# Forgetting attention with keys on the partitions, in slots with a written order on TensorE

## The chip, the cores and the metric

The kernel runs on one core of one Trainium2 chip. The metric is the device time of one execution in microseconds (us). A profile of one more execution tells, for each engine, when every instruction ran. The engines are TensorE (PE; its weight loads stand apart as PEld), VectorE (DVE), ScalarE (ACT), GpSimd (POOL) and SyncE (SP), which issues the DMA transfers.

## The reference, cut to what matters

One layer of a hybrid encoder, all in float32: 2048 positions, width 1024. A projection of the normalised input feeds three branches (forgetting attention, a state-space layer, attention into 256 memory tokens). Each is gated, projected back to 1024, and the three are merged with sigmoid gates; an output projection, the residual and a last norm follow. The change concerns the forgetting attention (12 heads of 64) and the merges.

```python
def forgetting_attention(q, k, v, log_f):
    F = jnp.cumsum(log_f, axis=1).transpose(0, 2, 1)
    ...
        s = jnp.einsum('bhqd,bhkd->bhqk', qi, kh)
        s = s + Fi[..., None] - F[:, :, None, :]
        s = jnp.where(key_pos[None, :] <= qpos[:, None], s, NEG)
        p = jax.nn.softmax(s, axis=-1)
        return jnp.einsum('bhqk,bhkd->bhqd', p, vh)
...
    gates = jax.nn.sigmoid(gl + b_merge[l]).reshape(Bn, L, N_BRANCH, D_MODEL)
    merged = (gates[:, :, 0] * (y_fox @ w_proj_fox[l])
              + gates[:, :, 1] * (y_s5 @ w_proj_s5[l])
              + gates[:, :, 2] * (y_mem @ w_proj_mem[l]))
```

The term F of the query is the same for all keys of a row, so softmax cancels it; only minus F of the key has to be added to the scores. Keys above the diagonal are masked.

## The kernel before, in words

Every product is made in float32 accuracy out of fp32r matmuls. `mm3` splits both factors into a high and a low part and makes three matmuls (lines 147 to 149). `split` makes the parts: high on POOL (line 893), or on ACT (line 891) once `hi_act` is set, and low on DVE (line 895). `load_w` loads a weight tile and splits it. Intermediate results go to DRAM and are loaded again, all by SP's queue.

The program has three stretches. `proj` makes all projections, the state-space and memory branches, and the gates of the first two chunks (a chunk is 512 positions, c = 0 to 3). Then comes attention (`gen_fox`) with a filler under it. Then the rest of the merges and the output projection (`merge_out`).

Attention before works with queries on the partitions. It goes through pairs of query blocks (head h, G = 7 to 0, 256 queries), in an order that mixes the small pairs of one head with the large ones of the next. `fox_scores` makes, for each block of 128 queries, the scores against up to 512 keys at a time with two matmuls (lines 751 and 752): the high and the low part of q against a tile that holds the high part of k in its upper 64 rows and the low part in its lower ones. One DVE operation (line 753) adds `nf` (minus F, broadcast over the partitions by a DMA), writes the row to SBUF and gives its maximum; POOL has added the mask into `nf` before (line 739). Then ACT takes the exponential with the row's sum (line 758), DVE the reciprocal (759), and POOL scales the row (762).

`fox_pv` does the pair before. TensorE transposes each 128x128 block of the row (line 783), ACT and DVE split what comes out into high and low (786 and 787; 791 and 792 on the diagonal), and a matmul of width 512 (line 799) multiplies both parts with a tile of values that holds high and low side by side. Lines 802 to 807 add the four quarters and multiply with the gate `gf`.

The filler is a generator that does six matmuls a step: first the gates of chunks 2 and 3 (`gen_gl`), then the merge of chunk 3 (`gen_merge0`), first its part without the attention's result, then, once `ready` is set, the part with it. `run` takes 0.355 of a step per step of attention, and holds it back behind a value matmul of eight steps before (`issue_after`). The Tile framework's scheduler otherwise orders the instructions of each engine by its own estimate of times, in the program's order where it can. What the filler has not done goes on after attention. `merge_out` then merges chunks 2, 1 and 0 with POOL adds on lines 997 and 998 (in `gen_merge0` the add is on line 963), and makes the output projection.

PSUM's eight banks are shared in this stretch as A 3, B 3, C 1 and F 1 (F is the filler's).

Of the kernel before, what the change touches and what calls it, by code (L numbers as in the profile page):

```python
# [33 lines left out]
PB, PBS = 4, 4  # L34
KS = 3
DUE = 6.0
QB = 2
PN = 768
# [11 lines left out]
class Layer:  # L50
# [17 lines left out]
    def setup(self):  # L68
# [19 lines left out]
        for n, sh, dt in (  # L88
            ("qh", [DF, L], F32), ("ql", [DF, L], F32), ("kh", [DF, L], F32), ("kl", [DF, L], F32),
            ("vs", [H, 16, 128, 128], F32), ("gf", [DF, L], F32), ("gs", [DF, L], F32),  # L90
            ("gl", [3 * D, L], F32), ("gm", [DM, L], F32), ("qmh", [DM, L], F32), ("qml", [DM, L], F32),
            ("u", [6, 8, 128, 256], F32), ("kd", [48, 16, 128], F32), ("nf", [H, L], F32), ("yx", [DF, L], F32), ("yc", [6, 8, 128, 256], F32),
            ("ys", [DF, L], F32), ("ym", [DM, L], F32), ("mp", [D, CW], F32), ("mg", [D, L], F32),
            ("mkh", [128, HM, ML], F32), ("mkl", [128, HM, ML], F32),
            ("mvh", [128, 2, DM], F32), ("mvl", [128, 2, DM], F32),
        ):
            s[n] = self.dram("s_" + n, sh, dt)
        self.s = s

    def constants(self):  # L100
# [6 lines left out]
        nc.sync.dma_start(out=self.bm, in_=i["b_merge"])  # L107
        self.bf = c.tile([H, 1], F32, name="bf")
# [35 lines left out]
    def mm3(self, out, a, b, first, last):  # L144

        nc = self.nc
        nc.tensor.matmul(out, a[0], b[0], start=first, stop=False)  # L147
        nc.tensor.matmul(out, a[0], b[1], start=False, stop=False)  # L148
        nc.tensor.matmul(out, a[1], b[0], start=False, stop=last)  # L149
# [106 lines left out]
    def proj_v(self, g, p):  # L256
# [6 lines left out]
        for t in range(16):  # L263
# [7 lines left out]
            o = self.ev.tile([128, 4, 128], F32R, tag="ehi", name="ev_v", bufs=2)  # L271
            pv = ps[:, :256].rearrange("p (h d) -> p h d", h=4)
            nc.scalar.copy(o[:, :, 0:64], pv)
            nc.vector.tensor_sub(o[:, :, 64:128], pv, fl32(o[:, :, 0:64]))
            nc.sync.dma_start(out=s["vs"][g * 4:(g + 1) * 4, t].rearrange("h p d -> p h d"), in_=fl32(o))
# [12 lines left out]
    def forget(self, p):  # L288
# [10 lines left out]
        nc.sync.dma_start(out=self.s["nf"], in_=e)  # L299
# [94 lines left out]
    def gen_gl(self):  # L394
        for n in range(len(TILES) - 24, len(TILES)):
            w = self.w_tile(n)
            for c in (2, 3):
# [6 lines left out]
                self.proj_chunk(*TILES[n], w, c, ps)  # L404
                yield
# [297 lines left out]
    def open_fox(self):  # L703
        self.fp, self.close_fp = self.pool("foxh", side="right")
        self.k0, self.q0 = [self.fox_keys(0, 0), self.fox_keys(0, 1)], self.fox_q(0, 3)

    def fox_keys(self, h, c):

        nc, s, p = self.nc, self.s, self.fp
        r, ks = slice(h * DH, (h + 1) * DH), slice(c * 1024, (c + 1) * 1024)  # L710
        kk = p.tile([128, 1024], F32R, tag="kk", name="kk", bufs=3)
        v = p.tile([128, 8, 128], F32R, tag="v", name="v", bufs=3)
        nf = p.tile([128, 1024], F32, tag="nf", name="nf", bufs=3)
        nc.sync.dma_start(out=fl32(kk[0:64]), in_=s["kh"][r, ks])
        nc.sync.dma_start(out=fl32(kk[64:128]), in_=s["kl"][r, ks])
        nc.sync.dma_start(out=nf, in_=s["nf"][h:h + 1, ks].partition_broadcast(128))
        nc.sync.dma_start(out=fl32(v), in_=s["vs"][h, c * 8:(c + 1) * 8].rearrange("t p d -> p t d"))
        return kk, v, nf

    def fox_q(self, h, c):  # L720
        nc, s, p = self.nc, self.s, self.fp
        r, cs = slice(h * DH, (h + 1) * DH), slice(c * 512, (c + 1) * 512)
        q = []
        for n in ("qh", "ql"):
            t = p.tile([128, 512], F32R, tag=n, name=n, bufs=QB)
            for a in range(2):
                nc.sync.dma_start(out=fl32(t[a * 64:(a + 1) * 64]), in_=s[n][r, cs])
            q.append(t)
        return q

    def fox_scores(self, p, hd, q, G, P):


        nc = self.nc
        for b in (1, 0):
            qb = 2 * G + b
            nk = 128 * (qb + 1)
            diag = hd[qb // 8][2][:, qb % 8 * 128:(qb % 8 + 1) * 128]
            nc.gpsimd.tensor_add(diag, diag, self.mask)
            qs = slice(qb % 4 * 128, (qb % 4 + 1) * 128)  # L740
            pr = p.tile([128, L // 2], F32, tag="Ps", name="Ps", bufs=PBS) if G < 4 else \
                p.tile([128, L], F32, tag="P", name="P", bufs=PB)
            nch = (nk + 511) // 512
            mx = p.tile([128, 4], F32, tag="mx", name="mx", bufs=4)
            for c in range(nch):
                w = min(512, nk - c * 512)
                wm = max(w, 256)
                kk, _, nf = hd[c // 2]
                c0 = c % 2 * 512
                ps = self.psA()  # L750
                nc.tensor.matmul(ps[:, :wm], q[0][:, qs], kk[:, c0:c0 + wm], start=True, stop=False)  # L751
                nc.tensor.matmul(ps[:, :wm], q[1][:, qs], kk[:, c0:c0 + wm], start=False, stop=True)  # L752
                nc.vector.tensor_tensor_reduce(  # L753
                    out=pr[:, c * 512:c * 512 + w], in0=ps[:, :w], in1=nf[:, c0:c0 + w], scale=1.0,
                    scalar=-3.0e38, op0=ALU.add, op1=ALU.max, accum_out=mx[:, c:c + 1])
            nm, den, rd = (p.tile([128, 1], F32, tag=n, name=n, bufs=4) for n in ("nm", "den", "rd"))
            nc.vector.reduce_max(nm, mx[:, :nch], axis=AX.X, negate=True)
            nc.scalar.activation(pr[:, :nk], pr[:, :nk], AF.Exp, bias=nm, accum_out=den)
            nc.vector.reciprocal(rd, den)  # L759
            for a in range(0, nk, PN):  # L760
                c = pr[:, a:min(a + PN, nk)]
                nc.gpsimd.tensor_scalar(out=c, in0=c, scalar1=rd, scalar2=0.5, op0=ALU.mult, op1=ALU.mult)  # L762
            P[b] = pr
            yield

    def fox_pv(self, p, h, hd, G, P):

        nc, s = self.nc, self.s
        po = self.psC()
        cs = slice(G * 256, (G + 1) * 256)  # L770
        r = slice(h * DH, (h + 1) * DH)
        gf = p.tile([64, 256], F32, tag="gf", name="gf", bufs=2)
        nc.sync.dma_start(out=gf, in_=s["gf"][r, cs])
        for kp in range(G + 1):
            ps = self.psB()
            t = p.tile([128, 2, 512], F32R, tag="Pt", name="Pt", bufs=3)
            hi, lo = t[:, :, 0:256], t[:, :, 256:512]
            for a in range(2):
                kt = 2 * kp + a
                for b in range(2):  # L780
                    if kt <= 2 * G + b:
                        o = a * 256 + b * 128
                        nc.tensor.transpose(ps[:, o:o + 128], P[b][:, kt * 128:(kt + 1) * 128], self.ident)  # L783
            psv = ps.rearrange("p (a n) -> p a n", a=2)
            if kp < G:
                nc.scalar.copy(hi, psv)  # L786
                nc.vector.tensor_sub(lo, psv, fl32(hi))  # L787
            else:
                for a in range(2):
                    c = slice(a * 128, 256)  # L790
                    nc.scalar.copy(hi[:, a, c], psv[:, a, c])
                    nc.vector.tensor_sub(lo[:, a, c], psv[:, a, c], fl32(hi[:, a, c]))
            for a in range(2):
                kt = 2 * kp + a
                v = hd[kt // 8][1][:, kt % 8, :]
                o, m = po, t[:, a, :]
                if kt == 2 * G + 1:
                    o, m = (z.rearrange("p (x b n) -> p x b n", x=2, b=2)[:, :, 1, :] for z in (o, m))
                self.pe = nc.tensor.matmul(o, v, m, start=(kt == 0), stop=(kt == 2 * G + 1))  # L799
            yield  # L800
        t = p.tile([128, 256], F32, tag="ot", name="ot", bufs=1)
        nc.scalar.copy(t, po[:, 256:512])
        nc.vector.tensor_add(t, po[:, 0:256], t)  # L803
        o = p.tile([64, 256], F32, tag="oo", name="oo", bufs=2)
        nc.scalar.copy(o, t[64:128])
        nc.gpsimd.tensor_add(o, o, t[0:64])
        nc.gpsimd.tensor_mul(o, o, gf)
        nc.sync.dma_start(out=s["yx"][r, cs], in_=o)

    def gen_fox(self):  # L810


        p, self.close_f = self.pool("fox", side="right")
        own = lambda h, a, b: [(h, G) for G in range(a, b, -1)]
        seq = own(0, 7, 7 - KS)
# [345 lines left out]
```

## Time and profile before

| | us |
|---|---|
| median of three runs | 3036.81 |
| lowest and highest | 3033.26, 3038.91 |
| the profiled execution's own time | 3032.29 |
| its span, first to last instruction | 3030.5 |
| PE, DVE, ACT, POOL busy | 2956.7, 1842.2, 1044.1, 864.8 |
| first score matmul (line 751) starts at | 1589.0 |
| last value matmul (line 799) starts at | 2513.4 |

A row of the profile names the engine, the line of the program, the operation, what it writes and reads, its shape and how often it ran; then the busy time, the mean time of one in ns, the idle time of the engine just before it, and what ended that idle time. A busy time is a union: two matmuls that overlap in the pipeline count once. A matmul's length includes its way through the array, so the price of one in a row of many is the distance between two starts. Rows of a single line's or tile's view give the shortest, median and longest time of one. The mean granted clock of TensorE was 0.992.

### The profile page before, as it was taken

How to read it: one execution, taken by the hardware profiler on the slowest of the kernel's cores; microseconds unless marked ns; L12 is line 12 of the kernel's file. 1: busy time of each engine (PE TensorE's matmuls, PEld its weight loads, DVE VectorE, ACT ScalarE, POOL GpSimd, SP SyncE). 2: the span in 40 equal slices, each digit the busy share in tenths (PEclk: the TensorE clock that was granted, in tenths of full speed). 3: DMA queues.
4: the chain of work that ended last, by engine and by line, in shares of the span. 5: the costliest groups of instructions: out<-in, count | busy, mean ns of one | idle time of the engine just before them, and what ended most of it. 6: DMA issues, size and time to landing. Idle time of an engine off the chain costs nothing.

```text
span 3030.5 us, 43647 instructions
## 1 busy us (share of the span) xinstructions
PE 2956.7 (98%) x14656; PEld 2424.2 (80%) x14656; DVE 1842.2 (61%) x4982; ACT 1044.1 (34%) x2049; POOL 864.8 (29%) x1160
## 2 busy tenths in 40 slices
PE   9999999999999999999999999999999897999999
PEld 7889977777777778888878888888888786788787
DVE  5333399899896673322216777777777875554444
ACT  5102111111112231222215666666666563332222
POOL 0010000000002342112215665565665662222100
PEclk9999999999999999999999999999999999999999
DMA  5343323323334655344352433444443548776542
GB/s 169 108 126 107 106 87 106 126 87 116 122 130 150 175 167 172 105 135 132 116 167 87 123 116 112 117 119 118 126 119 114 172 123 264 226 244 209 175 146 98
DMA packets 306671, 417.80 MB, mean 138 GB/s; under 512 B 84084, under 2 KB 165236, under 8 KB 306436
## 3 DMA queue, kind: packets, MB, share of 16 engines
q1 hardware_dynamic: 306160, 414.95, 44.9%
q8 instruction: 116, 1.90, 0.3%
q14 instruction: 107, 0.88, 0.1%
q10 hardware_dynamic: 288, 0.07, 0.0%
HBM read 276.00 MB, written 138.90 MB: 137 GB/s over the span
## 4 chain that ended last, share of the span: by engine, by line
PE 80%; DMA 9%; DVE 5%; issue 3%; POOL 2%; ACT 1%; SPq 0%; DVEq 0%; POOLq 0%; ACTq 0%
PE psF L147 10%; PE psF L148 10%; PE psF L149 10%; PE psA L149 8%; PE psA L147 8%; PE psA L148 8%; PE psC L799 6%; PE psB L783 5%; PE psA L752 3%; PE psA L751 3%; PE psC L147 2%; PE psC L149 2%; PE psC L148 2%; DMA wraw<-in_w_out 1%; DMA yr<-s_ys 1%
## 5 line engine op out<-in xcount | busy, mean ns | idle before, releaser
L147 PE MATMUL psF<-hh,whi 128*128 128x512 f32 (+1 forms) x1160 | 468.2, 404 | 5.5 <-DVE elo L228 2.5
L149 PE MATMUL psF<-hh,wlo 128*128 128x512 f32 (+1 forms) x1160 | 459.5, 396 | 0.0
L148 PE MATMUL psF<-hl,whi 128*128 128x512 f32 (+1 forms) x1160 | 459.1, 396 | 0.0
L893 POOL TENSOR_SCALAR whi<-wraw 128x1024 fp32r<-128x1024 f32 (+2 forms) x134 | 137.0, 1023 | 710.3 <-PE psA L148 307.0
L147 PE MATMUL psA<-hh,whi 128*128 128x512 f32 (+1 forms) x816 | 322.6, 397 | 2.5 <-POOL whi L893 1.5
L148 PE MATMUL psA<-hl,whi 128*128 128x512 f32 (+1 forms) x816 | 323.9, 397 | 0.0
L149 PE MATMUL psA<-hh,wlo 128*128 128x512 f32 (+1 forms) x816 | 321.8, 395 | 0.8 <-DVE wlo L895 0.8
L895 DVE TENSOR_TENSOR wlo<-wraw,whi 128x1024 fp32r<-128x1024 f32 (+2 forms) x168 | 204.9, 1221 | 191.8 <-POOL whi L893 152.5
L799 PE MATMUL psC<-Pt,v 128*128 128x512 f32 x864 | 266.1, 398 | 6.8 <-DVE ot L803 3.4
L787 DVE TENSOR_TENSOR Pt<-psB,Pt 128x512 fp32r<-128x512 f32 x336 | 226.4, 686 | 75.7 <-ACT Pt L786 73.2
L147 PEld LDWEIGHTS psF<-hh,whi 128*128 128x128 f32 x1160 | 218.6, 188 | 52.2 <-DVE elo L228 3.2
L149 PEld LDWEIGHTS psF<-hh,wlo 128*128 128x128 f32 x1160 | 218.4, 188 | 51.3 <-DVE wlo L895 0.4
L148 PEld LDWEIGHTS psF<-hl,whi 128*128 128x128 f32 x1160 | 218.7, 189 | 45.7 <-issue 0.4
L753 DVE CUSTOM_DVE_ANT_0 P<-psA,nf 128x512 f32<-128x512 f32 (+1 forms) x336 | 201.3, 627 | 45.7 <-PE psA L752 25.4
L786 ACT CAST Pt<-psB 128x512 fp32r<-128x512 f32 x336 | 191.7, 585 | 97.3 <-PE psB L783 52.4
L762 POOL TENSOR_SCALAR P<-P,rd 128x768 f32<-128x768 f32 (+1 forms) x240 | 192.1, 815 | 61.5 <-DVE rd L759 40.6
L751 PE MATMUL psA<-kk,qh 128*128 128x512 f32 (+1 forms) x480 | 185.1, 391 | 3.4 <-DVE mx L753 1.6
L147 PEld LDWEIGHTS psA<-hh,whi 128*128 128x128 f32 x816 | 154.0, 189 | 38.0 <-POOL whi L893 1.9
L149 PEld LDWEIGHTS psA<-hh,wlo 128*128 128x128 f32 x816 | 154.4, 189 | 35.9 <-DVE wlo L895 1.2
L148 PEld LDWEIGHTS psA<-hl,whi 128*128 128x128 f32 x816 | 154.4, 189 | 33.4
L799 PEld LDWEIGHTS psC<-Pt,v 128*128 128x128 f32 x864 | 153.8, 190 | 33.7 <-DVE Pt L787 5.6
L783 PE MATMUL psB<-ident,P 128*128 128x128 f32 x1200 | 176.3, 273 | 0.3
(373 smaller groups left out, 6243.1 us busy)
## 6 DMA issues: line engine op xcount, KB each, us to landing
wraw<-in_w_in SPq DMA_DIRECT2D x90, 512.0 KB, 4.1
s_gl<-ehi SPq DMA_DIRECT2D x96, 256.0 KB, 2.6
g<-s_gl SPq DMA_DIRECT2D x96, 256.0 KB, 4.6
wraw<-in_w_proj SPq DMA_DIRECT2D x40, 320.0 KB, 4.0
s_vs<-ev_v SPq DMA_DIRECT2D x48, 256.0 KB, 2.7
nf<-s_nf SPq DMA_DIRECT2D x24, 512.0 KB, 6.6
v<-s_vs SPq DMA_DIRECT2D x24, 512.0 KB, 6.1
qh<-s_qh SPq DMA_DIRECT2D x96, 128.0 KB, 3.7
```

The lines of the kernel that those rows point to most:

```text
L147: nc.tensor.matmul(out, a[0], b[0], start=first, stop=False)
L148: nc.tensor.matmul(out, a[0], b[1], start=False, stop=False)
L149: nc.tensor.matmul(out, a[1], b[0], start=False, stop=last)
L751: nc.tensor.matmul(ps[:, :wm], q[0][:, qs], kk[:, c0:c0 + wm], start=True, stop=False)
L753: nc.vector.tensor_tensor_reduce(out=pr[:, c * 512:c * 512 + w], in0=ps[:, :w], in1=nf[:, c0:c0 + w], scale=1.0, scalar=-3.0e38, op0=ALU.a ...
L762: nc.gpsimd.tensor_scalar(out=c, in0=c, scalar1=rd, scalar2=0.5, op0=ALU.mult, op1=ALU.mult)
L783: nc.tensor.transpose(ps[:, o:o + 128], P[b][:, kt * 128:(kt + 1) * 128], self.ident)
L786: nc.scalar.copy(hi, psv)
L787: nc.vector.tensor_sub(lo, psv, fl32(hi))
L799: self.pe = nc.tensor.matmul(o, v, m, start=(kt == 0), stop=(kt == 2 * G + 1))
L893: self.nc.gpsimd.tensor_scalar(out=hi, in0=x, scalar1=sc, scalar2=1.0, op0=ALU.mult, op1=ALU.mult)
L895: self.nc.vector.tensor_sub(lo, x, fl32(hi))
```

## The change

Attention is written anew, with keys on the partitions. A unit is a head and a chunk of 512 queries; the units go from chunk 3 to chunk 0, and through all heads in each. A slot is one tile of 128 keys of a unit: 16, 12, 8 or 4 slots a unit, 480 in all, and 13 more at the end.

In each slot two matmuls make the scores of 128 keys against up to 512 queries (`fox_score`). ACT copies them out of PSUM with minus F of the key added as its bias into a tile `T` (four key tiles each, six buffers), and DVE keeps a running maximum over the key tiles, from PSUM; on the diagonal POOL adds the mask to `T`, and DVE takes the maximum from there. When a unit's scores are done, four transposes and a DVE reduction give the maximum of each query (`fox_max`), ACT spreads it, and four more transposes put it on all partitions (`rows`, a PSUM bank of its own). Then `fox_exp`, two key tiles at a time: DVE adds the negated maximum from PSUM, ACT takes the exponential, POOL adds each tile to a running sum `acc`. `fox_pv` multiplies the exponentials with the values, in plain float32 (no split), the key tiles taking turns between the lower and the upper 64 partitions of the result. Four matmuls with a column of ones make the sums of each query out of `acc` (`fox_den`), and `fox_end` applies their reciprocals and the gate.

What follows a unit's scores is put at fixed slots behind them (`at`), so it runs between the scores of the next units. Every PE instruction of attention and filler goes through `te`, which chains it behind the one before in the order of the program. The filler now does the gates of chunks 2 and 3 and both parts of the merges of chunks 3 and 2, 0.67 steps a slot; chunk 2 waits until its 24 units are done. Weight tiles are loaded one ahead. `merge_out` keeps chunks 1 and 0. Minus F is transposed once (`forget`) and stays in SBUF; values are no longer split. The PSUM banks become A 2, B 1, C 2, F 2 and M 1.

```diff
-PACE, LAG = 0.355, 8
+PACE = 0.67
-PS2 = {"A": 3, "B": 3, "C": 1, "F": 1}
+PS2 = {"A": 2, "B": 1, "C": 2, "F": 2, "M": 1}
...
+    def te(self, op, *a, **k):
+        f = getattr(self.nc.tensor, op)
+        if not self.chain:
+            return f(*a, **k)
+        with self.tc.issue_after(self.pe.ins) if self.pe else nullcontext():
+            self.pe = f(*a, **k)
...
+    def fox_score(self, p, u, kt):
...
+        self.te("matmul", ps[:, w:], kk[:, ks], q[0][:, w:], start=True, stop=False)
+        self.te("matmul", ps[:, w:], kk[:, ks], q[1][:, w:], start=False, stop=True)
+        nc.scalar.activation(t[:, a:], ps[:, a:], AF.Identity, bias=bias)
+        if j >= 0:
+            nc.gpsimd.tensor_add(t[:, a:a + 128], t[:, a:a + 128], self.mask)
+            if kt:
+                nc.vector.tensor_max(mx[:, a:], mx[:, a:], t[:, a:])
+            else:
+                nc.vector.tensor_copy(mx, t)
+        elif kt:
+            nc.vector.scalar_tensor_tensor(out=mx, in0=ps, scalar=bias, in1=mx, op0=ALU.add, op1=ALU.max)
+        else:
+            nc.vector.tensor_scalar(out=mx, in0=ps, scalar1=bias, scalar2=None, op0=ALU.add)
...
+    def fox_exp(self, p, u, g, i):
...
+        if g < c:
+            t = tg[:, i:i + 2, :]
+            nc.vector.tensor_add(t, m.unsqueeze(1).to_broadcast([128, 2, CW]), t)
+            nc.scalar.activation(t, t, AF.Exp)
+        for e in (i, i + 1):
+            t, a = tg[:, e, :], 128 * e if g == c else 0
+            if g == c:
+                nc.vector.tensor_add(t[:, a:], m[:, a:], t[:, a:])
+                nc.scalar.activation(t[:, a:], t[:, a:], AF.Exp)
+            if g or e:
+                nc.gpsimd.tensor_add(acc[:, a:], acc[:, a:], t[:, a:])
+            else:
+                nc.gpsimd.tensor_copy(acc, t)
...
+        for kt in range(4 * g, 4 * g + 4):
+            t, a = u["T"][g][:, kt % 4, :], max(kt - 4 * c, 0) * 128
+            o = u["po"][64 * (kt % 2):64 * (kt % 2) + 64, a:]
+            self.te("matmul", o, u["v"][:, kt, :], t[:, a:], start=kt < 2, stop=kt >= 4 * c + 2)
...
+        for b in range(4):
+            self.te("matmul", pd[:, b:b + 1], u["acc"][:, b * 128:(b + 1) * 128], self.ones, start=True, stop=True)
...
+        seq = [(h, c) for c in range(NC - 1, -1, -1) for h in range(H)]
...
+            at = lambda d, f, *a: due.setdefault(slot - 1 + d, []).append(lambda: f(*a))
+            at(1, self.fox_values, p, u)
+            at(2, self.fox_max, p, u)
+            at(4, rows, u)
+            for g in range(c + 1):
+                for i in range(2):
+                    at(4 + 4 * g + 2 * i, self.fox_exp, p, u, g, 2 * i)
+                at(9 + 4 * g, self.fox_pv, u, g)
+            at(11 + 4 * c, self.fox_den, p, u)
+            at(13 + 4 * c, self.fox_end, p, u)
...
     def gen_merge0(self):
...
+        slabs = [(c, m, a) for c in (3, 2) for b in ((0, 1), (2,)) for m in range(KD) for a in b]
...
+        for _ in range(8):
+            yield
+        for c in (3, 2):
...
+                if part == 0 and c == 2:
+                    while self.done < 2 * H:
+                        yield
...
     def merge_out(self):
...
-        for c in range(NC - 2, -1, -1):
+        for c in (1, 0):
...
-        for n, _ in enumerate(fox):
-            marks.append(self.pe)
+        for _ in fox:
             due += PACE
             while due >= 1.0:
                 due -= 1.0
...
+                next(fill, None)
```

More of the change, by code (lines that the diff above doesn't have):

```diff
@@ L1 @@
+from contextlib import nullcontext
 import concourse.bass as bass
@@ L144, in mm3 @@
     def mm3(self, out, a, b, first, last):
[L146 to L149, printed above, removed]
+        self.te("matmul", out, a[0], b[0], start=first, stop=False)
+        self.te("matmul", out, a[0], b[1], start=False, stop=False)
+        self.te("matmul", out, a[1], b[0], start=False, stop=last)
+    def te(self, op, *a, **k):
[4 more added lines that the diff above has]
+            self.pe = f(*a, **k)
     def rsqrt(self, p, out, ssq, n):
@@ L298, in forget @@
         nc.vector.tensor_tensor_scan(e, one.to_broadcast([H, L]), z, 0.0, ALU.mult, ALU.subtract)
-        nc.sync.dma_start(out=self.s["nf"], in_=e)
+        pz = self.psB()
+        for t in range(16):
+            nc.tensor.transpose(pz[:, t * H:(t + 1) * H], e[:, t * 128:(t + 1) * 128], self.ident[0:H, 0:H])
+        nc.scalar.copy(self.nf, pz[:, :16 * H].rearrange("p (t h) -> p t h", h=H))
     def proj_kv(self, p):
@@ L720, in fox_q @@
[L720 to L725, printed above, removed]
-            for a in range(2):
[L727 to L787, printed above, removed]
-            else:
[L789 to L806, printed above, removed]
@@ new lines, in fox_rows @@
+    def fox_rows(self, u, ps, n):
+        for b in range(4):
+            self.te("transpose", ps[:n, b * 128:(b + 1) * 128], u["x"][:, b, :n], self.ident)
+        return ps
+    def fox_exp(self, p, u, g, i):
+        nc, c = self.nc, u["c"]
+        tg = u["T"][g]
+        if g == 0 and i == 0:
+            u["acc"] = p.tile([128, CW], F32, tag="acc", name="acc", bufs=2)
+        acc, m = u["acc"], u["m"]
+        if g < c:
[11 more added lines that the diff above has]
+                nc.gpsimd.tensor_copy(acc, t)
@@ L845, in gen_fox @@
+        while due:
+            run()
+            slot += 1
             yield
@@ L913, in merge_gate @@
         return t
-    def merge_w(self, m, part, pool=None):
-        return [self.load_w(self.i["w_proj"][2 * m + a], (5, 128)) for a in range(2)] if part == 0 else \
-            [self.load_w(self.i["w_proj_x"][m], (6, 128))]
     def merge_ws(self, m, p):
@@ L1074, in run @@
                 due -= 1.0
-                if n >= LAG and marks[n - LAG] is not None:
-                    with self.tc.issue_after(marks[n - LAG].ins):
-                        next(fill, None)
-                else:
-                    next(fill, None)
-        self.over = self.hi_act = True
+                next(fill, None)
+        self.hi_act = True
         for _ in fill:
             pass
+        self.chain = False
         self.close_f()
```

244 lines of the change are left out of this document (142 added, 102 removed).

## Prediction, made before the changed kernel was run

> **What bounds the kernel now.** I read the page's busy times first, then the busy times of three stretches of the span, then single stretches of time for the price of each kind of matmul.
>
> ```profile
> span 3030.5 us, 43647 instructions
> PE 2956.7 (98%) x14656; PEld 2424.2 (80%) x14656; DVE 1842.2 (61%) x4982; ACT 1044.1 (34%) x2049; POOL 864.8 (29%) x1160
> 0.00:1589.00 1589.00, 1564.91 (x7744) 1281.84 (x7744) 902.11 (x2527) 327.94 (x648) 212.94 (x307) 0.99 0.42 129
> 1589.00:2520.00 931.00, 914.81 (x4898) 760.68 (x4899) 688.06 (x2045) 579.23 (x1164) 563.26 (x800) 0.99 0.42 122
> 2520.00:3031.00 511.00, 476.93 (x2015) 381.64 (x2014) 251.99 (x411) 136.97 (x237) 88.64 (x55) 0.98 0.61 194
> ```
>
> The last three rows give, after each stretch's length, the busy time of PE, PEld, DVE, ACT and POOL, then clock and DMA. The stretches are what comes before attention (1589 us, which the change hardly touches), attention with the fill under it (931 us), and what is left of the merges with the output projection (510.5 us to the end). PE is busy almost throughout all three, so I count the change in PE time first and then ask whether another engine takes over. In attention DVE is at 74% and POOL at 60%.
>
> **Prices on PE.** A busy time overlaps its neighbours, so I take prices from the distance of starts.
>
> ```profile
> 2012.56 1.55 PE L799 MATMUL psC<-Pt,v 128*128 128x512 f32 x6
> 2018.37 0.60 PE L783 MATMUL psB<-ident,P 128*128 128x128 f32 x4
> 405.35 0.48 PE L149 MATMUL psA<-hh,wlo 128*128 128x512 f32 x1
> 405.76 1.08 PE L586 MATMUL psC<-u,m1t 128*64 128x256 f32 x8
> 406.78 0.33 PE L551 MATMUL psB<-ident,m1i 128*128 128x128 f32 x1
> 418.14 0.60 PE L626 MATMUL psC<-u,m 128*128 128x256 f32 x2
> 418.58 0.59 PE L627 MATMUL psC<-hs,z 128*128 128x256 f32 x2
> L799 PE MATMUL psC<-Pt,v 128*128 128x512 f32 x768 | 240.3, 408 | 6.8 <-DVE ot L803 3.4 <-DVE Pt L787 2.9 <-DVE Pt L792 0.2
> L799 PE MATMUL psC<-Pt,v 128*128 128x256 f32 x96 | 30.0, 313 | 0.0
> L783 PE MATMUL psB<-ident,P 128*128 128x128 f32 x1200 | 176.3, 273 | 0.3
> L783 PE MATMUL psB<-ident,Ps 128*128 128x128 f32 x432 | 65.9, 272 | 0.1
> ```
>
> A 512-wide fp32r matmul costs (1.55-0.39)/5 = 0.233 us, with 0.39 the length of one; a transpose (0.60-0.27)/3 = 0.11 us. A plain fp32 matmul leaves two records: two of 256 columns take 418.58-418.14 = 0.44 us, 0.217 each. The S5 block on L586 is four fp32 matmuls (eight records) whose outputs alternate between the lower and upper 64 partitions, which is the form of the new value product. One after another they would be 8 x 0.217 = 1.74 us. From the end of the matmul before (405.83) to the end of the block (406.84) it took 1.01 us, and the transpose behind it 0.26 instead of 0.11. So neighbours in different halves run together: 0.86 us of work and 0.30 us for entering and leaving.
>
> The Trainium skill (TensorEngine Tiling (Array Packing), Key Properties) says that a change of tiling mode drains TensorE. With no drain the sum below would be 36 us lower; the trace's 0.30 us per block agrees with the page.
>
> **PE time out and in.** Out: 768 value matmuls x 0.233 + 96 half-wide ones x 0.12 = 190 us, and 1632 transposes x 0.11 = 178 us. Scores stay: 80 matmuls a head with the same widths, only their operands swap sides. In, for each of 48 units (head h, 512 queries c): value products in groups of four key tiles. A full group is four steps of 0.433 (twice 0.217) + 0.30 = 2.03 us; a diagonal group, whose widths are 512, 384, 256 and 128, is 2 x 0.433 + 2 x 0.217 + 0.30 = 1.60. With 72 full and 48 diagonal groups: 223 us. Twelve transposes a unit: 576 x 0.11 = 63 us. Four one-column denominator matmuls a unit, which no row shows: not below one transpose (0.11), not above a two-record matmul (0.43); I take 0.22, two 128-column passes, as the weight load must still pass: 192 x 0.22 = 42 us (21 to 83). In total 368 out, 328 in: 40 us less.
>
> Merges moved under attention:
>
> ```profile
> 2520.00:3031.00 511.00, 266.66 (x671) 127.43 (x671) 0.98 0.61 194
> 2520.00:3031.00 511.00, 266.65 (x672) 127.75 (x671) 0.98 0.61 194
> 2520.00:3031.00 511.00, 264.96 (x672) 127.59 (x672) 0.98 0.61 194
> PE psA L147 <- ACT whi L891: 8.0, 1, 8.0
> PE psB L147 <- ACT ymg L891: 5.4, 3, 2.9
> PE psC L147 <- DVE g L996: 4.8, 2, 4.2
> ```
>
> The first three rows are lines 147, 148 and 149 in the last stretch: 2015 matmuls. Chunks 1 and 0 need 2 x 384 and the output 768, so 1536 stay and 479 move: 479 x 0.233 = 112 us. Moving does not shorten them. The last three rows are the largest waits of that stretch, at the start of the merges and at a change of chunk. I keep them whole: the new merge_out opens its buffers only when attention's are closed, so its first weights and y tiles still have to land and be split (minus 15 to plus 10 us). Last stretch: 510.5-112 = 398.5. Attention, if PE alone sets it and stalls stay as they are: 931-40+112 = 1003. With 1589 that is 2990.5, 40 us under the span. The 16 small transposes in forget (1.8 us) and the dropped value splitting (DVE, beside PE) I cost at nothing: PE is busy for 1565 of 1589 us there and covers them; uncovered they would be 2 us.
>
> **What POOL and DVE get.** The new path puts one running sum per key tile on POOL, 128x512, two inputs.
>
> ```profile
> 2599.51 0.82 DVE L895 TENSOR_TENSOR wlo<-wraw,whi 128x640 fp32r<-128x640 f32 x1
> 2600.25 1.93 DVE L895 TENSOR_TENSOR lob<-raw,hib 128x640 fp32r<-128x640 f32 x1
> 2599.68 1.82 POOL L997 TENSOR_TENSOR g<-g 128x512 f32<-128x512 f32 x1 [30.59 <-DVE g L996]
> 2841.05 1.29 POOL L997 TENSOR_TENSOR g<-g 128x512 f32<-128x512 f32 x1 [5.64 <-DVE g L996]
> L806 POOL TENSOR_TENSOR oo<-oo,ot x96: 714/731/1715, 1627.1 to 2517.9; 64x256 f32<-64x256 f32 x96
> L739 POOL TENSOR_TENSOR nf<-nf,mask x192: 444/459/1437, 1550.6 to 2495.7; 128x128 f32<-128x128 f32 x192
> L893 POOL TENSOR_SCALAR ymg<-yr x10: 607/618/1099, 2354.6 to 2382.4; 128x512 fp32r<-128x512 f32 x10
> L893 POOL TENSOR_SCALAR whi<-wraw x134: 714/1046/1798, 9.2 to 2483.0; 128x1024 fp32r<-128x1024 f32 x96, 128x768 fp32r<-128x768 f32 x24, 128x640 fp32r<-128x640 f32 x14
> L895 DVE TENSOR_TENSOR ymg<-yr,ymg x64: 674/693/2861, 2355.2 to 2696.9; 128x512 fp32r<-128x512 f32 x64
> L895 DVE TENSOR_TENSOR lob<-raw,hib x24: 810/820/1928, 2531.5 to 2821.1; 128x640 fp32r<-128x640 f32 x24
> L787 DVE TENSOR_TENSOR Pt<-psB,Pt 128x512 fp32r<-128x512 f32 x336 | 226.4, 686 | 75.7 <-ACT Pt L786 73.2
> ```
>
> One POOL add of 512 columns is 1.29 us alone, 1.82 when it starts 0.65 us before a DVE operation with two SBUF inputs ends. The next such DVE operation starts inside the POOL add, and takes 1.93 instead of 0.82: it ends 0.68 after the add. So the two exclude one another. A DVE operation that reads PSUM does not: POOL's median over attention (0.731, 0.459) is near its minimum though DVE is busy 74% of the time.
>
> So POOL's work and DVE's two-SBUF work add up, as if on one engine. POOL per unit: adds of 1.29 per full tile (the first is a copy, 0.62), 1.29+1.01+0.73+0.46 on the diagonal (384 columns interpolated), four masks 1.82, the final product 1.29: 21.4 us for c=3, 16.2 for c=2, 11.1 for c=1, 6.0 for c=0. DVE's maxima on the diagonal are two-SBUF: about 1.9 a unit (1.7 for c=0). The fill's merges: weight hi parts 36 us, 42 y tiles x 0.62 = 26, 32 adds x 1.29 = 41 on POOL; on DVE the low parts, 41 + 42 x 0.69 = 70.
>
> The fill runs at 0.67 steps a slot; the 192 steps of the gates and 8 empty ones end near slot 299 of 493. Two parts of attention follow:
> First part (12 units of c=3, 9 of c=2, gates): PE 12 x 16.7 + 9 x 12.9 + 1152 x 0.233 = 585 us; POOL and two-SBUF DVE 12 x 21.4 + 9 x 16.2 + 25 + 41 + 29 = 498. PE leads.
> Second part (3 units of c=2, 12 of c=1, 12 of c=0, 768 merge matmuls): PE 3 x 12.9 + 12 x 9.0 + 12 x 5.1 + 179 = 387. POOL 3 x 16.2 + 12 x 11.1 + 12 x 6.0 + 103 = 357, two-SBUF DVE 49 + 70 = 119, together 476. The pair leads by 89 us. A handover overlaps (0.65 us of overlap cost 0.53), about 0.13 for some 200 of them, 27 us at most: 62 to 89. DVE as a whole has there some 358 us (PSUM operations at 0.686 for 512 columns, 1.22 to 1.37 for 1024) and waits of half a POOL operation before most of 198 two-SBUF ones, some 80 us: 440, also above PE.
>
> The Trainium skill (GPSIMD Engine Reference, Specifications) names the same forms: GpSimd contends with DVE instructions that have two SBUF inputs or run in a two-port mode. Were every DVE instruction excluded, the second part would want 357 + 358 = 715 us instead of 476; the medians above speak against that, with the page.
>
> Behind a late POOL stand the diagonal mask, then DVE's maximum, then the transposes of the maximum, two slots after the last score; TensorE's order is written out, so the fill behind them waits too. What hid POOL until now is that PE was slower; in the second part it is not.
>
> **The sum.** 2990.5 + 68 (near the lower end of 62 to 89, since part of the old stalls lies in it) = 3058 us of span. The profiled execution's time is 3032.3 for a span of 3030.5, and the median of the runs is 3036.8: plus 6.3, so 3064.
>
> **Rivals.** *PE stays the bound* (0.37): POOL's sums find room because POOL may lag, and six T buffers hold it; over all of attention POOL and two-SBUF DVE want 974 us against 972 of PE. For it: the old kernel hid 563 us of POOL with 33 us of PE stalls. Against it: the mask lets POOL lag two slots only. Then 2990.5+6.3 = 2997, faster; stalls that the fixed order removes too would bring it to 2970. It decides if POOL and two-SBUF DVE need under some 420 us in the second part (34 us over PE's 387).
> *DVE's lag stops the short units* (0.10): at c=0 the single psB bank is asked for in three of every four slots, each time waiting for a DVE reader. If DVE lags over one slot (2.2 us), each costs 1 to 2 us: 12 x 3 x 1.5 = 54 on top, 3118.
> *The halves do not run together* (0.03) in the new product: 72 x 1.73 + 48 x 0.87 = 166 us more than PE's count, 3163. The S5 block speaks against it.
> *The two effects cancel* (0.07): the two engines need 34 to 46 us more than PE there, which gives back the 40 us: 3031 to 3043.
>
> **How the numbers follow.** The forecast (port bound in the second part) has 0.43, with a range of its own from 3035 to 3100. About 0.2% is what a measurement of this kernel tells from no change. Faster is the first rival, 0.37; same the last, 0.07; slower the forecast and the two others, 0.56. The range must reach into the first rival and the second: 2968 to 3130.
>
> **What would show it.** Right: the stretch from the last gate matmul to the end of attention has PE well below 95% busy and POOL with DVE's two-SBUF lines filling it; POOL's 512-column add has a mean over 1.4 us; PE waits for readers that stand behind POOL's mask or DVE. The value product in a full group takes near 2.0 us, its records seven ns apart in pairs; 1632 transposes become 576. Wrong: PE at 98% throughout attention, an attention stretch under 1010 us, or value matmuls that follow one another at 0.43 us.

## The result and the profile after

The changed kernel takes 3232.86 us (median of four runs, 3224.58 to 3236.68), the kernel before beside it 3036.61: a ratio of 1.0644, 95% interval 1.062 to 1.0667. It is slower, by 196 us where 27 were forecast. The head of the page after, and the busy times by stretch (length, then PE, PEld, DVE, ACT, POOL, granted clock, DMA share, GB/s):

```profile
span 3222.4 us, 41372 instructions
PE 2998.0 (93%) x14096; PEld 2312.9 (72%) x14096; DVE 1942.0 (60%) x3975; ACT 1035.0 (32%) x1840; POOL 1104.7 (34%) x1214
```

```profile
0.00:1587.10 1587.10, 1565.12 (x7760) 1282.30 (x7760) 887.57 (x2480) 329.84 (x649) 212.32 (x306) 0.99 0.41 124
1587.10:2308.70 721.60, 618.97 (x2701) 422.66 (x2701) 446.94 (x588) 377.90 (x589) 424.57 (x416) 0.92 0.36 98
2308.70:2827.20 518.50, 447.56 (x2098) 314.07 (x2096) 423.19 (x578) 227.87 (x421) 409.87 (x458) 0.92 0.59 170
2827.20:3222.40 395.20, 366.40 (x1540) 293.85 (x1540) 184.33 (x330) 99.41 (x182) 57.95 (x36) 0.97 0.57 175
```

The four stretches are what comes before attention, attention up to the first merge matmul (the prediction's first part), attention with merges (its second part), and the rest. Attention is 1240 us, 1071 were forecast. The outer stretches are as forecast (1587 and 395 us). In both parts PE is busy only 86% of the time, and the clock is 0.92 where it was 0.99. TensorE's clock was halved for 109 us of the first part and 85 us of the second, and it was busy for 80 and 71 of these; at half speed that is some 40 and 35 us of lost work.

What TensorE waits for in the first part (us in total, times, longest), and in the second:

```profile
PE psA L155 <- DVE mx L757: 99.6, 27, 6.4
```

```profile
PE psA L155 <- DVE mx L757: 25.2, 10, 5.6
PE psB L155 <- DVE mx L753: 24.3, 21, 3.7
PE psB L155 <- DVE gf L839: 6.7, 7, 2.8
PE psB L155 <- ACT xb L772: 5.4, 7, 1.6
```

Nearly all of the first part's waits are one wait: TensorE wants a score bank, and DVE's running maximum (line 757) has not yet read it. The timeline of one such wait, in unit c=3 (start, length, engine, line):

```profile
1855.50 6.88 DVE L789 TENSOR_TENSOR T<-psM,T 128x1024 f32<-128x1024 f32 x6 [0.21 <-PE psM L155]
...
1858.46 0.69 ACT L749 ACTIVATE T<-psA,nf 128x512 f32<-128x512 f32 x1
...
1859.03 0.40 PE L155 MATMUL psF<-hh,wlo 128*128 128x512 f32 x1
...
1862.30 1.68 DVE L794 TENSOR_TENSOR T<-psM,T 128x512 f32<-128x512 f32 x4
...
1863.89 0.74 DVE L757 SCALAR_TENSOR_TENSOR mx<-psA,nf,mx 128x512 f32<-128x512 f32 x1
...
1864.69 0.80 PE L155 MATMUL psA<-qh,kk 128*128 128x512 f32 x1 [5.26 <-DVE mx L757]
...
1865.71 0.63 PE L155 MATMUL psF<-hh,whi 128*128 128x512 f32 x1
...
1866.13 0.63 PE L155 MATMUL psF<-hl,whi 128*128 128x512 f32 x1
```

`fox_exp` is written two key tiles at a time, between the next unit's scores. But as soon as `rows` has put the maxima into psM (1855.50), DVE does all ten of the unit's subtractions in one run, 8.5 us, while the next scores' maxima stand behind them. ACT reads the second of the two full score banks at 1858.46; DVE's maximum for the first comes only at 1863.89. Meanwhile TensorE, whose order is written out, stands for 5.26 us. Afterwards the same matmuls start 0.42 us apart instead of 0.233. Two windows of the same view as above show the clock, before this wait and just at it:

```profile
1831.40:1862.00 30.60, 28.03 (x128) 18.10 (x126) 17.14 (x21) 15.07 (x23) 11.62 (x15) 1.00 0.42 112
1862.00:1869.00 7.00, 4.31 (x13) 3.55 (x13) 4.63 (x9) 4.01 (x7) 6.61 (x6) 0.51 0.01 2
```

### The profile page after: what moved, and what is told of

The parts are those of the page before. It is cut to its first block, busy times and chain, and to the rows that moved or that the text cites. A ratio compares the mean times of both kernels' runs of the same rounds, so it can differ in the third digit from the quotient of the medians.

```text
span 3222.4 us, 41372 instructions
## 1 busy us (share of the span) xinstructions
PE 2998.0 (93%) x14096; PEld 2312.9 (72%) x14096; DVE 1942.0 (60%) x3975; ACT 1035.0 (32%) x1840; POOL 1104.7 (34%) x1214
## 4 chain that ended last, share of the span: by engine, by line
PE 70%; DVE 11%; DMA 7%; POOL 5%; issue 5%; ACT 2%; SPq 0%; DVEq 0%; POOLq 0%; ACTq 0%
PE psA L153 21%; PE psF L153 20%; PE psF L155 9%; PE psA L155 5%; PE psC L153 4%; PE psC L155 3%; DVE T L789 3%; POOL acc L797 3%; PE psB L153 2%; PE psB L155 2%; DVE T L794 1%; DMA wraw<-in_w_out 1%; DVE mx L753 1%; DVE mx L757 1%; DVE wlo L933 1%
## 5 line engine op out<-in xcount | busy, mean ns | idle before, releaser
L797 POOL TENSOR_TENSOR acc<-acc,T 128x512 f32<-128x512 f32 (+3 forms) x432 | 497.2, 1151 | 23.2 <-ACT T L790 1.5
L749 ACT ACTIVATE T<-psA,nf 128x512 f32<-128x512 f32 x480 | 293.5, 623 | 475.7 <-PE psA L155 444.6
L155 PE MATMUL psA<-qh,kk 128*128 128x512 f32 x480 | 215.7, 450 | 134.1 <-DVE mx L757 124.8
L153 PE MATMUL psF<-hh,whi 128*128 128x512 f32 (+1 forms) x776 | 308.4, 397 | 4.0 <-DVE elo L234 2.5
L153 PE MATMUL psF<-hh,wlo 128*128 128x512 f32 (+1 forms) x776 | 308.1, 397 | 0.1
L757 DVE SCALAR_TENSOR_TENSOR mx<-psA,nf,mx 128x512 f32<-128x512 f32 x252 | 188.3, 747 | 121.3 <-ACT T L749 115.8
L155 PE MATMUL psC<-T,v 128*64 128x512 f32 (+1 forms) x960 | 212.2, 544 | 0.0
L155 PE MATMUL psA<-ql,kk 128*128 128x512 f32 x480 | 184.1, 385 | 0.0
L155 PE MATMUL psF<-ymg,whi 128*128 128x512 f32 x512 | 175.8, 427 | 0.0
L789 DVE TENSOR_TENSOR T<-psM,T 128x1024 f32<-128x1024 f32 x144 | 166.4, 1216 | 13.0 <-PE psM L155 12.9
```

The source lines that it names most:

```text
L153: return f(*a, **k)
L155: self.pe = f(*a, **k)
L749: nc.scalar.activation(t[:, a:], ps[:, a:], AF.Identity, bias=bias)
L757: nc.vector.scalar_tensor_tensor(out=mx, in0=ps, scalar=bias, in1=mx, op0=ALU.add, op1=ALU.max)
L789: nc.vector.tensor_add(t, m.unsqueeze(1).to_broadcast([128, 2, CW]), t)
L797: nc.gpsimd.tensor_add(acc[:, a:], acc[:, a:], t[:, a:])
```

## The experiments

Unit lengths below are the distances between first scores of successive units, medians over the twelve heads; "first" and "second part" are bounded as above; time at half clock is added up from the trace's clock records. A run without an interval is a single execution; four executions of one kernel lie up to 0.5% (15 us) apart, so small differences of totals tell little there. The kernel before took 3041 to 3042 us beside these runs.

**VectorE's order written out too.**

```diff
+    def ch(self, eng, op, *a, **k):
+        f = getattr(getattr(self.nc, eng), op)
+        if eng not in ORDERED:
+            return f(*a, **k)
+        last = self.last.get(eng)
+        with self.tc.issue_after(last.ins) if last else nullcontext():
+            self.last[eng] = f(*a, **k)
...
-            nc.vector.scalar_tensor_tensor(out=mx, in0=ps, scalar=bias, in1=mx, op0=ALU.add, op1=ALU.max)
+            self.ch("vector", "scalar_tensor_tensor", out=mx, in0=ps, scalar=bias, in1=mx, op0=ALU.add, op1=ALU.max)
```

Every DVE operation of attention goes through `ch`; the subtractions of the last head of a chunk stay free, since the next chunk's units are shorter.

> Attention's DVE operations are put in the order of the slots (each behind the one before in the program, issue order only; the exponentials of the last head of each chunk stay free). Theory 'order': in the changed kernel DVE takes all subtractions of a unit's maximum in one run (six of 1.21 us and four shorter) ahead of the running maxima of the next scores, the two psA banks stay full, PE waits some 5 us once a unit and its clock is halved for 7 to 10 us behind it. Then c=3 units fall from 40 to 32-34 us, PE's waits for the running maximum (line 757 there, 125 us) to under 25 us, and the time from 3233 to 3080-3120. Theory 'sums' (the prediction's: POOL's running sums with DVE's two-SBUF operations are the bound): under 20 us of change, 3210-3235.

Measured: 3161.54 us, ratio 1.04 (1.0383 to 1.0417) to before. The two parts by stretch, and DVE alone in the timeline of a c=3 unit:

```profile
1584.30:2213.20 628.90, 592.08 (x2700) 395.73 (x2701) 442.18 (x584) 376.51 (x584) 430.76 (x412) 0.99 0.41 113
2213.20:2765.70 552.50, 454.25 (x2098) 314.35 (x2096) 412.62 (x581) 235.33 (x426) 408.83 (x462) 0.91 0.55 159
```

```profile
1781.22 0.75 DVE L165 SCALAR_TENSOR_TENSOR mx<-psA,nf,mx 128x512 f32<-128x512 f32 x1 [2.78 <-ACT T L162]
1781.89 1.21 DVE L165 TENSOR_TENSOR T<-psM,T 128x1024 f32<-128x1024 f32 x1
1783.02 0.74 DVE L165 SCALAR_TENSOR_TENSOR mx<-psA,nf,mx 128x512 f32<-128x512 f32 x1
```

The subtractions now stand between the maxima. With the same DVE work (442 us for 447) the first part falls from 722 to 629 us, the c=3 unit from 40.3 to 32.9, the clock is 0.99 again. TensorE's waits for the running maximum fall from 125 to 28 us over all attention, not quite under the 25 named. That part of the theory holds. The total missed the 3080 to 3120 because the second part grew by 34 us.

**No running sums.** `acc` is set to one and the adds of `fox_exp` are left out, so the denominators are not computed.

```diff
-            if g or e:
-                nc.gpsimd.tensor_add(acc[:, a:], acc[:, a:], t[:, a:])
-            else:
-                nc.gpsimd.tensor_copy(acc, t)
+            if not (g or e):
+                nc.gpsimd.memset(acc, 1.0)
```

> POOL's running sums are left out (a memset of ones takes the first one's place), so the output is not divided by the sums of the exponentials; nothing else changes. 497 us of POOL's work go. Theory 'order': c=3 units stay at 39-41 us, since the run of DVE operations is as long as before; only the waits for the mask in the last part shrink, 3190-3230. Theory 'sums': the second part of attention falls to PE's own 387 us or near it, by 70 to 130 us, 3100-3160.

Measured: 3193.06 us, by stretch:

```profile
1586.30:2306.80 720.50, 625.33 (x2700) 429.21 (x2701) 435.57 (x589) 377.86 (x589) 109.33 (x153) 0.91 0.37 98
2306.80:2794.80 488.00, 432.69 (x2098) 303.58 (x2096) 369.74 (x577) 227.99 (x421) 224.71 (x289) 0.95 0.63 180
```

GpSimd's work in the first part falls from 425 to 109 us, and the part stays at 720: with VectorE's order left free, GpSimd does not set it. The second part falls by 31.

**Three score banks** (the filler gives one).

```diff
-PS2 = {"A": 2, "B": 1, "C": 2, "F": 2, "M": 1}
+PS2 = {"A": 3, "B": 1, "C": 2, "F": 1, "M": 1}
```

> The score banks psA become three, the filler's psF one. Theory 'order': the third bank lets PE go on for one more slot (2 us) in each run of DVE operations; of 100 us of waits in the first part 45 to 60 go and the halved clock with some of them; one psF bank costs up to 0.7 us a gate tile, 30 us: 3150-3210. Theory 'sums': no gain, 3230-3270.

Measured: 3203.79 us; the first part 687, the c=3 unit 37.4. Its waits in the first part:

```profile
PE psA L155 <- DVE mx L757: 58.4, 34, 4.5
```

One bank more covers a part of the 8.5 us run: the wait falls by 41 us and does not go. The second part rises to 532, with waits for the single psF bank.

**VectorE's order and no sums**, both edits above.

> DVE in the order of the slots as in the first run, and POOL's running sums left out (ones in their place, so no division by them). If both theories hold a part, this falls below the first run by what POOL's load costs once the order is mended: 40 to 90 us by the prediction's count of the second part, to 2990-3050. If the order is all there is, it stands within 15 us of the first run.

Measured: 3066.15 us.

```profile
1584.90:2192.10 607.20, 588.37 (x2701) 400.54 (x2702) 419.42 (x585) 375.63 (x584) 106.17 (x154) 0.98 0.43 117
2192.10:2666.80 474.70, 422.60 (x2098) 295.39 (x2096) 362.63 (x581) 233.78 (x426) 219.26 (x289) 0.97 0.64 185
```

Beside the ordered kernel, the sums cost 22 us in the first part and 78 in the second. The miss against 2990 to 3050 is that the second part stays 88 us over PE's 387 even without them.

**High parts of the splits on ScalarE** from the start of attention, with VectorE in order.

```diff
-        self.chain = True
+        self.chain = self.hi_act = True
```

> The kernel with the attention's VectorE work in slot order (3162 us, its second part 552 us) and, from the start of the attention on, the high parts of the merges' splits on ScalarE instead of GpSimd. It computes the same. Theory 'GpSimd's queue in the second part': leaving the running sums out took the second part from 552 to 475 us, so taking some 60 us of splits from the same engine gives back a good part of it: second part about 500 us, the whole 3105 to 3125 us. Rival 'VectorE's fixed order alone': the second part is long because short units wait for VectorE's turn, GpSimd's splits do not matter: 550 us, 3155 to 3170 us. Rival 'ScalarE': it takes on 60 us and the copies and exponentials become late: over 3175 us.

Measured: 3146.62 us, the second part 531 us for 552. It lies between the theories: 60 us less work on GpSimd gave 22. TensorE's waits for ScalarE's `xb` in psM grew over all attention from 13.6 us in the ordered kernel to 25.0 here; that they ate the rest is not shown.

**VectorE's order for c=3 and c=2 only.**

```diff
-        if eng not in ORDERED:
+        if eng not in ORDERED or self.free:
...
+            self.free = c < 2
```

> VectorE's work in slot order only for the units of the last two chunks (c=3 and c=2); the units of c=1 and c=0 leave it to the scheduler as the changed kernel does. It computes the same. The changed kernel has 722 us in the first part and 519 in the second, the kernel in order throughout 629 and 552. Theory 'the fixed order helps long units and holds up short ones': 629 and about 520, the whole 3125 to 3140 us. Rival 'the second part is long for what the first left behind': 629 and 550, 3155 to 3170 us.

Measured: 3140.03 us; first part 632, second 525. As the first theory says, most of the loss, 27 of the 34 us, came from the written order in the short units.

**Later slots for short units**, with VectorE in order.

```diff
-            at(1, self.fox_values, p, u)
+            d = 4 if c < 2 else 0
+            at(1 + d, self.fox_values, p, u)
...
-                at(9 + 4 * g, self.fox_pv, u, g)
+                at(9 + d + 4 * g, self.fox_pv, u, g)
```

> VectorE's work in slot order, and for the units of c=1 and c=0 the later steps moved back on TensorE: values and exponentials by two to four slots, value products, denominators and the end of a unit by four. It computes the same. Theory 'tight slots': in the short units TensorE comes to a step before VectorE, GpSimd and ScalarE have finished what it needs, a matter of latency; with four slots more the second part falls from 552 to 490 to 520 us, the whole 3100 to 3130 us. Rival 'work': the engines beside TensorE have too much to do in the second part, later slots change nothing: 545 to 560 us, 3155 to 3175 us.

Measured: 3158.00 us, the second part 543 for 552: nearly nothing, and within the spread of single runs in the total. Four slots of slack are not what is missing.

**TensorE left to the scheduler too.** Unlike in the kernel before, nothing then holds the filler back behind attention.

```diff
-        self.chain = True
         fox = self.gen_fox()
```

> The changed kernel with one part of the change undone: TensorE's attention instructions are no longer held to the written order of slots, the scheduler places them as it places VectorE's. It computes the same. Theory 'mismatch': what costs is a written order on TensorE beside a free one on VectorE; with both free they fit better, the c=3 units fall from 40.3 us to under 37, and the whole comes to 3080 to 3190 us. Rival 'the new form itself': keys on the partitions cost VectorE and GpSimd so much that any order gives the same, 40 us a unit and 3215 to 3245 us. Rival 'the written order is worth something': without it TensorE waits for each unit's own exponentials, units of 45 us and more, over 3280 us.

Measured: 3297.64 us. TensorE's wait for line 757 falls from 124.8 us to 18.0 over all attention, so a free order on both fits there. But the scheduler drew the filler forward: the first merge matmul comes at 1966 us instead of 2309. The c=3 units, and the rest of attention:

```profile
1587.20:2183.90 596.70, 560.52 (x2367) 381.50 (x2368) 332.06 (x413) 251.70 (x381) 304.75 (x293) 0.97 0.39 113
2183.90:2902.30 718.40, 601.77 (x2432) 356.91 (x2430) 537.15 (x757) 355.87 (x628) 532.09 (x584) 0.83 0.45 128
```

In the first row TensorE has 662 matmuls more than the changed kernel has in its c=3 units (2367 for 1705), 154 us at 0.233 each, which the second row lacks. That row has a clock of 0.83: some 122 us lost to it in 718. The written order on TensorE, which also keeps the filler in its place, is worth 65 us here. The third theory has the time right, but its reason is the smaller part (28 waits for exponentials, 32 us); the larger, as these rows read, is that the filler is spread over the short units.

**Idle work in the wait.**

```diff
+        if c == 3 and h and kt == 5:
+            d = self.psF()
+            for _ in range(22):
+                self.te("matmul", d, kk[:, 0:128], q[0], start=True, stop=True)
         ps = self.psA()
```

> The changed kernel with idle work on TensorE: in each c=3 unit but the first, 22 matmuls of 512 columns (22 x 0.233 = 5.1 us at full clock) into a bank that nothing reads, just before the sixth score, where TensorE waits some 5 us for VectorE. The output is not touched. Theory 'the wait brings the half clock': the added work lies in the wait, the clock stays full after it, so of the 109 us at half clock in the first part most go, the c=3 units fall from 40.3 to 35.5 to 38 us, the first part from 722 to 670 to 695, the whole 3180 to 3205 us. Rival 'the clock falls for another reason': the units stay at 40 to 41 us, half-clock time about 109, the whole 3222 to 3245. Rival 'the added work is not hidden': units of 43 us and more, the whole over 3255 us.

Measured: 3211.52 us. The c=3 units by stretch, here and (second fence) in the changed kernel:

```profile
1584.20:2038.70 454.50, 433.92 (x1947) 304.30 (x1947) 274.68 (x360) 236.06 (x365) 262.26 (x251) 0.98 0.35 94
```

```profile
1587.10:2054.80 467.70, 402.81 (x1705) 276.68 (x1705) 274.90 (x360) 237.20 (x365) 259.05 (x251) 0.91 0.34 91
```

With 242 matmuls (56 us) more, the twelve units are 13 us shorter. Time at half clock in them falls from 85 us to 20, TensorE's idle time from 65 to 21. The halved clock is thus a consequence of the wait. The gain is smaller than expected (unit 38.2 us, not 35.5 to 38), as part of the added work lay outside the waits.

**The merges behind the attention**, with VectorE's order for c=3 and c=2.

> The kernel with VectorE's order fixed for c=3 and c=2 (3140 us, first part to the first merge matmul 632, second 525), its merges of the last two chunks run after the attention, not under it. It computes the same. Theory 'shared engines': under the short units the merges' splits and sums on GpSimd and VectorE hold the units up about as much as the merges' matmuls fill TensorE's waits; alone the c=1 units fall from 22 to 17 or 18 us and the c=0 units to about 9, the merges take 140 to 170 us behind them, and the whole stays at 3120 to 3160 us. Rival 'the overlap is worth its price': c=1 units stay at 20 us or more, the merges come on top, 3190 us and more. Rival 'the overlap only costs': under 3110 us.

```diff
-            yield from self.gen_merge0()
...
         for _ in fill:
             pass
+        for _ in self.gen_merge0():
+            pass
         self.chain = False
```

Measured: 3264.42 us. The c=1 units, the c=0 units, and most of the merges alone:

```profile
2301.00:2512.00 211.00, 155.21 (x632) 90.85 (x630) 164.13 (x222) 119.91 (x210) 149.56 (x163) 0.80 0.32 86
2512.00:2636.00 124.00, 96.83 (x490) 64.70 (x486) 83.55 (x156) 65.19 (x142) 85.88 (x133) 0.83 0.37 110
2636.00:2870.00 234.00, 194.10 (x747) 146.67 (x748) 98.46 (x128) 56.61 (x83) 41.05 (x27) 0.93 0.67 206
```

The units do fall, as the first theory has it (17.1 us at c=1, 8.7 on average at c=0); but the third row's 234 us hold 689 of the merges' 768 matmuls, where 140 to 170 us were expected for all. The whole is 124 us longer than with the merges under attention (3140 us), so the overlap is worth that. The rows that matter for the prediction are the first two: with nothing beside them the short units take 335 us, where PE's prices give 12 x 9.0 + 12 x 5.1 = 169. No engine is busy throughout, and the clock is 0.80 and 0.83. TensorE's largest wait in the c=1 units is the one of the first part again, 41.8 of its 56 idle us: five of the unit's six subtractions stand in one run ahead of a running maximum. (Line 162 is the helper `ch` where it leaves the order free.)

```profile
PE psA L156 <- DVE mx L162: 41.8, 23, 4.1
```

```profile
2448.69 3.75 DVE L162 TENSOR_TENSOR T<-psM,T 128x1024 f32<-128x1024 f32 x5 [0.41 <-PE psM L156]
2452.36 0.74 DVE L162 SCALAR_TENSOR_TENSOR mx<-psA,nf,mx 128x512 f32<-128x512 f32 x1
```

**The two mends together**: VectorE's order for c=3 and c=2, high parts on ScalarE.

> The kernel with VectorE's order fixed for c=3 and c=2, and the high parts of the merges' splits on ScalarE from the start of the attention on. It computes the same. Each of the two took some 15 to 22 us from the kernel in order throughout, at different places. Theory 'they add up': second part about 505 us, the whole 3115 to 3130 us, still some 2.6% over the kernel before. Rival 'the same wait': 3135 to 3145 us, as one alone. Rival 'ScalarE is late': over 3150 us.

Measured: 3120.32 us, ratio 1.0248 (1.0223 to 1.0273) to before; first part 633, second 503. The second part falls by 27 and 22 us from the ordered kernel's 552, so the two add up. It is the fastest full version of the new form that was found, and slower than the kernel before.

**A second bank for transposes and denominators** in the changed kernel.

```diff
-PS2 = {"A": 2, "B": 1, "C": 2, "F": 2, "M": 1}
+PS2 = {"A": 2, "B": 2, "C": 2, "F": 1, "M": 1}
```

> The changed kernel with a second bank for the transposes and denominators (psB 2), taken from the filler (psF 1), as the run with three score banks took one. It computes the same. The changed kernel's waits for the one psB bank are 24.3 + 6.7 + 5.4 = 36 us in the second part (519 us); the run with psA 3 and psF 1 had 532 there, with 28.6 us of waits for psF. Theory 'the one psB bank stops the short units' (the rival of the prediction with 0.10): those waits go, the second part falls to 480 to 500 us and the whole to 3200 to 3215 us, although psF costs something. Rival 'VectorE is late, the bank only shows it': TensorE waits for the same results at the next bank, the second part stays at 515 to 535 us, the whole 3225 to 3250 us.

Measured: 3240.87 us, the second part 552 us for 519, with these waits in it:

```profile
PE psB L155 <- DVE mx L753: 34.2, 22, 3.4
PE psF L155 <- DVE g L1006: 25.5, 20, 4.3
PE psA L155 <- DVE mx L757: 19.4, 12, 6.4
```

The wait for line 753 is still there: it is for the maximum itself, not for the bank. The wait for `gf` (6.7 us) is gone from the list, and the filler's single bank costs more than that.

## Why the prediction was wrong, step by step

**Prices on PE: right.** One full value group of the changed kernel (four products, eight records) with its neighbours:

```profile
1831.84 0.39 PE L155 MATMUL psA<-ql,kk 128*128 128x512 f32 x1
1832.07 0.60 PE L155 MATMUL psB<-ident,xb 128*64 128x128 f32 x4
1832.60 1.94 PE L155 MATMUL psC<-T,v 128*64 128x512 f32 x8
1834.47 0.50 PE L155 MATMUL psA<-qh,kk 128*128 128x512 f32 x1
1834.81 0.40 PE L155 MATMUL psA<-ql,kk 128*128 128x512 f32 x1
```

The group ends 1.87 us after the transposes (1834.54 and 1832.67), and the score behind it another 0.43 instead of 0.233 later: 2.06 us, forecast 2.03. The halves run together, so that rival falls. The four denominator matmuls, which no row had shown, take 0.81 us from the start of one such group (1664.40) to the score behind it (1665.21), 0.20 each for the 0.22 taken. The last stretch came to 395 us for 398.5, and the outer 1587 us are unchanged: the 112 us of moved merges were counted rightly too.

**"First part ... PE leads" (585 us): this is the step that failed.** The sum had 585 + 387 us of PE, 31 of old stalls and 68 for GpSimd and DVE, 1071 in all; the two parts took 722 and 518, and the first of them is most of the miss. The sum weighed each engine's total work, found PE ahead, and assumed that what PE waits for would be there. But TensorE's order had been written out and DVE's had not, and DVE took a unit's subtractions in one run. In order, the same work takes 629 us; without sums as well 607, which is PE's 585 and 22 us, within the 31 us of old stalls kept for both parts. Of the 137 us missed here, 93 are DVE's order. None of the rivals was this one; the nearest, *DVE's lag*, looked for late reads at the psB bank of the short units, not at the score banks of the long ones.

**PE at full clock: a term that the sum lacked.** All prices were those of a clock of 0.99. The 75 us of lost work given above lie within the excess of both parts (169 us over the 1071); the idle work in the wait shows that, in the c=3 units, most of it follows the waits. The trace has eleven episodes of half clock in these units, one for each wait of 4.9 to 6.4 us or pair of waits of 3.2 to 3.9 (TensorE's waits under 1.5 us there brought none), and they last 3.4, 6.8 or 10.2 us. The Trainium skill (TensorE: Matmul & The Clock Gate, HAM oscillation) warns of TensorE gaps over some 3.4 us that bring the half clock back; in the c=3 units the trace agrees, and the page should have stood among the rivals as the price of any wait. In the second part the measurement goes beyond it: eleven of the fifteen half-clock episodes there follow waits of at most 3.0 us, only four a longer one.

**GpSimd and VectorE exclude one another in the second part (68 us): place and sign right, but the size not confirmed, and not the whole.** Leaving the sums out gives 31 us in the changed kernel, under half of the 68, and 78 with VectorE in order; both take away the adds themselves and not only their clash with VectorE, so neither is the price of the exclusion alone. Groups of the second part (line, operation, count; busy, mean ns):

```profile
L797 POOL TENSOR_TENSOR acc<-acc,T 128x512 f32<-128x512 f32 x80 | 114.8, 1435 | 2.5 <-ACT T L790 0.4
L933 DVE TENSOR_TENSOR ymg<-yr,ymg 128x512 fp32r<-128x512 f32 x34 | 41.9, 1233 | 7.0 <-POOL ymg L931 7.0
```

And all of line 789, which reads PSUM (shortest, median, longest):

```profile
L789 DVE TENSOR_TENSOR T<-psM,T x144: 1208/1215/1226, 1613.5 to 2668.1; 128x1024 f32<-128x1024 f32 x144
```

GpSimd's add has 1.435 us for 1.29 alone, DVE's two-SBUF subtraction 1.233 for 0.674 at its shortest before; the operation with a PSUM input never varies by more than 18 ns. That is the exclusion as predicted, and PE is at 86%, well below the 95% named. But GpSimd and DVE's two-SBUF lines (753 and 933) together, overlaps counted once, are busy for 433 of the 518 us: they do not fill the part, as a bound would. And the 387 us of PE under it were too low a floor: 475 remain without any sums. That the c=1 and c=0 units alone take twice PE's price, at a clock of 0.80 and 0.83, points to the round from TensorE over ACT, GpSimd's mask, DVE and back, not to PE's work. In the c=1 units the failed step returns there: DVE's run of subtractions ahead of a maximum. In the c=0 units TensorE waits most for the diagonal's maximum, which stands behind GpSimd's mask (15.2 of 27 idle us). But DVE's written order made the short units longer, and four later slots, a third score bank and a second psB bank each left the second part at 532 to 552 us, so what would shorten this round stays open.

That the change came out slower, as forecast, is for the larger part luck: of the 196 us, leaving the sums out takes back 40, and the forecast's reason does not reach the first part at all.

**The rivals.** *PE stays the bound* (2997) fell: PE waits 14% of attention. (Its 33 us of PE stalls in the old attention are not in the rows, which have 931.00 us with PE busy for 914.81, so 16; it fell for the new waits all the same.) *DVE's lag stops the short units* named waits that are there (36 us for psB in the second part) but the wrong cause: most are for line 753's maximum itself, and a second bank does not remove them. *The two effects cancel* fell with the forecast.

## What to carry to other kernels

Where one engine's order is written out, look at the order of the engines that feed it: total work per engine says which could bound, and only the order of each queue says whether buffers of two deep are enough for the longest run of other work ahead of a release. Here the written order on DVE gained 93 us in the long units and lost 27 in the short ones, so it is no rule for both. Price a wait of TensorE at the wait plus work at half clock behind it: the c=3 units had 65 us of idle time and 85 us at half clock. Where units get short, price the round through all engines once: the c=1 and c=0 units alone took 335 us for 169 of PE's prices.

## What the runs showed of the hardware that was not expected

The half clock comes in whole steps of 3.4 us: of eleven episodes in the c=3 units two had one step, four two, five three, after waits of 3.2 to 6.4 us. Adding 56 us of matmuls nobody reads made these units 13 us shorter. And attention alone, with its engines 53 to 78% busy, ran its short units at a clock of 0.80 and 0.83 with single waits of no more than 4.1 us, only one of them over 3.4.
